# Retention in a two-layer hybrid trunk: outputs parked in their queries' place, normalised two tiles at a time, transposed five steps on, and the PSUM bank `o` used in halves

## The chip, the cores and the metric

The kernel runs on one core of a Trainium2 chip. The metric is device time in microseconds (us) for one execution; a kernel's time is the median of its runs. One more execution was taken with the hardware profiler, and every row shown here comes from it.

## The reference, cut to what matters

The program is one inference step of a trunk of two layers over 1280 tokens: 1024 latent tokens and 256 context tokens, 1024 channels, float32. Every layer normalises and modulates its input, multiplies it by one wide input matrix, runs three token mixers side by side (a retention of 4 heads in both directions, grouped-query attention, latent attention), multiplies their outputs by a gate, and projects back. The change lies in the retention, and in a PSUM bank that retention and both attentions share. What the retention must give, for each chunk of 128 tokens:

```python
def step(s, inp):
    qi, ki, vi = inp
    a = jnp.einsum('bihd,bjhd->bhij', qi, ki) * intra
    o = (jnp.einsum('bhij,bjhe->bihe', a, vi)
         + jnp.einsum('bihd,bhde->bihe', qi, s) * q_dec[None, :, :, None])
    s = s * c_dec[None, :, None, None] + jnp.einsum('bjhd,bjhe->bhde', ki * k_dec[None, :, :, None], vi)
    return s, o
...
o = rms_norm(o_f + jnp.flip(o_b, 1))      # over the 64 columns of each head
```

## The kernel before

The tokens are 10 tiles of 128 rows (`NT` = 10; tiles 0 to 7 latent, 8 and 9 context). One SBUF tensor `yxs` holds all of them; `yx[t]` is tile t, 1024 columns wide, and its first 256 columns hold the retention's queries until the retention's output takes their place.

A layer's second half of the input projection is the gate: `z_blk` runs four times, each with two column blocks by three token blocks (512, 512 and 256 tokens), and each such block is 24 matmuls (lines 685 to 687) into a bank `acc`. Scalar engine then takes a tanh (line 690) and vector engine a product (line 692) out of that bank, in two halves. These matmuls need nothing from the mixers, so other work is woven between them: `aside()` is a generator, and `z_blk` draws one step from it after, and in wide blocks also in the middle of, each block, 40 draws in all. What it yields in order: the rest of the key transposes, the latent keys and values (`latents`), the retention (10 steps that gather the states `S`, then the steps t = 0, 1, 2, ... of the main loop), and the attention's preparation (loads and splits of its first keys and values, then the first three score jobs, lines 1249 and 1250), three of its steps at a draw. A scheduler orders the instructions of each engine by priority and by its own estimate of when their inputs are there; each engine then runs its list strictly in that order, and waits on semaphores.

One step t of the retention's main loop works on three tiles:

- `stage_c(t-2)`: eight pairs of small matmuls (lines 905, 906) put the outputs of tile t-2 into the left half of PSUM bank `o`; scalar engine squares them into the right half (line 907); vector engine sums the squares per head (909), computes the reciprocal root by Newton steps on 128x4 elements (`newton`, lines 152 to 162: 13 small instructions), and multiplies the outputs by it into an SBUF tile `oret` (912). The next tile's outputs go into the same bank.
- `stage_b(t-1)`: two matmuls (895) give the scores of tile t-1; vector engine multiplies them by the decay mask into `At` (897).
- `stage_a(t)`: gpsimd has doubled the queries into `qq` (401); PE transposes them (870) and the keys (873), vector engine makes the decayed queries `qdT` (877), scalar engine copies queries and keys into `BD` and `kT` (879, 880, 882). In the free half of the keys' bank PE transposes `oret` of tile t-3 (`stage_d`, 918), and scalar engine copies it to `yx` (919).

The banks `pt`, `pk` and that of line 895 come from one ring `tp` of two banks, so the key transposes of step t (873) take the bank out of which line 897 reads the scores of tile t-1. `qq` and `At` share a ring `kd` of three buffers.

In the attention, `pv_job` accumulates the outputs of one head over two token tiles in the left half of bank `o` (lines 1313, 1314); scalar engine copies 64 of its rows (1325) and vector engine adds the other 64 (1326). Then the next pair of tiles may start in that bank.

Of the kernel before, what the change touches and what calls it, by code (L numbers as in the profile page):

```python
# [10 lines left out]
F32 = mybir.dt.float32  # L11
# [7 lines left out]
P = 128  # L19
# [63 lines left out]
def hybrid_trunk(tc, I, O):  # L83
# [51 lines left out]

    def bank(tag):
        if tag == "o":
            return pp.tile([P, 512], F32, name=tag, tag=tag, bufs=1)
        if tag == "m":
            tag = "tp"  # L140
        bufs = {"acc": NACC, "tp": 7 - NACC}[tag]
        return pp.tile([P, 512], F32, name=tag, tag=tag, bufs=bufs)
# [647 lines left out]
    def retention(l, rt, load, kv):  # L790
# [76 lines left out]
        def stage_a(t, kv, qq):  # L867
# [6 lines left out]
            if t >= 3:  # L874
                stage_d(t - 3, outs.pop(t - 3), pk[:, 256:512])
# [24 lines left out]
        def stage_c(t, kv, qdT, At):  # L900
            bo = bank("o")
            po, sq = bo[:, 0:256], bo[:, 256:512]
            for h in range(4):
                hs = slice(h * 64, (h + 1) * 64)
                T.matmul(po[:, hs], At[:, h, :], kv[:, 256 + h * 64:256 + (h + 1) * 64], start=True, stop=False)  # L905
                T.matmul(po[:, hs], qdT[:, h, :], S[:, t, hs], start=False, stop=True)  # L906
            A.activation(sq, po, AF.Square)
            ss = sm.tile([P, 4], F32, name="ss4", tag="ss4")
            V.tensor_reduce(ss, h4(sq), axis=AX.X, op=ALU.add)
            rstd = newton(ss, 4, 1.0 / 64)  # L910
            o = rt.tile([P, 256], F32, name="oret", tag="cur", bufs=2)
            V.tensor_tensor(h4(o), h4(po), bc(rstd), op=ALU.mult)
            return o

        def stage_d(t, o, pt):

            for i in range(2):
                T.transpose(pt[:, i * 128:(i + 1) * 128], o[:, i * 128:(i + 1) * 128], ident)
            A.copy(yx[t][:, 0:256], pt)

        st, At, outs = {}, {}, {}
        for t in range(NT + 3):
            yield
            if 2 <= t < NT + 2:
                outs[t - 2] = stage_c(t - 2, st[t - 2][0], st[t - 2][1], At.pop(t - 2))
# [8 lines left out]
            elif t >= 3:  # L934
                stage_d(t - 3, outs.pop(t - 3), bank("tp")[:, :256])
# [126 lines left out]
    def attention(l, att):  # L1062
# [207 lines left out]
        def exp_job(p, i, b, ps):  # L1270
# [3 lines left out]
            if b == p.nb - 1 and i == 1:  # L1274
                if p.i not in ris:
                    ris[p.i] = sm.tile([P, 5, 2, 2], F32, name="ri", tag="ri", bufs=3)
# [27 lines left out]
        def pv_job(p, b, c0, c1):  # L1304
            if b == 0 and c0 == 0:
                p.po = bank("o")[:, :256]
# [415 lines left out]
```

## Time and profile before

| | us |
|---|---|
| median of 3 runs | 2138.68 |
| lowest and highest run | 2135.28 and 2139.26 |
| the profiled execution | 2134.77 |
| its span, first to last instruction | 2133.0 |

The profiled execution is 3.9 us below the median, about as far as the lowest run. Of its time 1.8 us lie outside the span.

| engine | busy us | share of the span |
|---|---|---|
| PE (TensorE matmul) | 2064.7 | 97% |
| DVE (vector) | 1489.9 | 70% |
| ACT (scalar) | 1177.9 | 55% |
| POOL (gpsimd) | 992.8 | 47% |

The granted TensorE clock was 0.994 of full speed as a mean, and 1.00 in the stretches spoken of here. Each engine's idle time is put down to what ended it, so that a row of the waits says who waited, on which line, for whom, how long in total, how many times, and the longest. The retention's main part lies at 405 to 487 us of the span in the first layer and at 1430 to 1515 us in the second.

### The profile page before, as it was taken

The numbers are of one execution on the slowest core, as the hardware profiler recorded it, in microseconds if no ns is written. First come the engines' busy times: TensorE is split into PE (matmuls) and PEld (weight loads), VectorE is DVE, ScalarE is ACT, GpSimd is POOL, SyncE is SP. The second block draws the span as 40 slices with busy tenths as digits, with TensorE's granted clock in tenths as the row PEclk, the third lists the DMA queues.
The fourth block names the chain that finished last, engine by engine and source line by source line (L and its number), as shares of the span: only waits on it lengthen the run. The fifth ranks groups of instructions, "written<-read, shape, count | busy, mean of one in ns | idle before, by whom it ended". The sixth has DMA issues, their size and how long they took to land. (4 is left out here: it accounts for less than half of the span.)

```text
span 2133.0 us, 42211 instructions
## 1 busy us (share of the span) xinstructions
PE 2064.7 (97%) x14798; PEld 1854.8 (87%) x14798; DVE 1489.9 (70%) x3780; ACT 1177.9 (55%) x3190; POOL 992.8 (47%) x1444
## 2 busy tenths in 40 slices
PE   6999999999999999999999999998999999999998
PEld 3899987778888888888999999887788888888898
DVE  4625584566999999997174358546699999999824
ACT  3503333225888888885253233322388888888623
POOL 2342242325676565544543224223275766564474
PEclk9999999999999999999999999999999999999999
DMA  9442436414111110014143212452321111010322
GB/s 323 138 150 60 132 105 197 137 49 121 34 52 34 31 48 27 24 35 149 41 157 106 62 55 57 135 148 74 98 61 30 40 48 41 12 40 24 108 94 100
DMA packets 203814, 179.94 MB, mean 84 GB/s; under 512 B 37532, under 2 KB 186324, under 8 KB 203604
## 3 DMA queue, kind: packets, MB, share of 16 engines
q1 hardware_dynamic: 202164, 172.01, 26.9%
q10 hardware_dynamic: 1440, 5.24, 0.6%
q8 instruction: 118, 1.93, 0.4%
q14 instruction: 92, 0.75, 0.1%
HBM read 131.32 MB, written 45.86 MB: 83 GB/s over the span
## 5 line engine op out<-in xcount | busy, mean ns | idle before, releaser
L258 PE MATMUL acc<-wh,ah 128*128 128x256 f32 (+1 forms) x1760 | 504.0, 286 | 1.8 <-ACT ah L406 1.8
L260 PE MATMUL acc<-wh,al 128*128 128x256 f32 (+1 forms) x1760 | 500.5, 284 | 2.6 <-DVE al L407 2.4
L259 PE MATMUL acc<-wl,ah 128*128 128x256 f32 (+1 forms) x1760 | 501.7, 285 | 0.0
L1258 DVE TENSOR_REDUCE nm<-acc 128x1 f32<-128x512 f32 (+1 forms) x624 | 413.7, 666 | 47.1 <-PE acc L1252 34.0
L1297 PE MATMUL tp<-ident,pn 128*128 128x128 f32 x2400 | 433.6, 274 | 3.9 <-DVE pT L1302 2.3
L1302 DVE TENSOR_TENSOR pT<-tp,pT 128x512 fp32r<-128x512 f32 (+1 forms) x624 | 412.7, 663 | 27.8 <-ACT pT L1301 19.4
L1272 ACT ACTIVATE pn<-acc,nm 128x512 f32<-128x512 f32 (+1 forms) x624 | 421.2, 682 | 10.2 <-DVE nm L1263 9.3
L1301 ACT CAST pT<-tp 128x512 fp32r<-128x512 f32 (+1 forms) x624 | 356.4, 573 | 122.9 <-PE tp L1297 117.5
L258 PEld LDWEIGHTS acc<-wh,ah 128*128 128x128 f32 x1760 | 335.1, 190 | 13.1 <-issue 7.8
L260 PEld LDWEIGHTS acc<-wh,al 128*128 128x128 f32 x1760 | 333.5, 190 | 4.9 <-DVE al L407 4.3
L259 PEld LDWEIGHTS acc<-wl,ah 128*128 128x128 f32 x1760 | 334.3, 190 | 0.8 <-issue 0.8
L1313 PE MATMUL o<-pT,V 128*128 128x256 f32 x1200 | 326.2, 293 | 1.5 <-DVE yx L1326 1.5
L1297 PEld LDWEIGHTS tp<-ident,pn 128*128 128x128 f32 x2400 | 287.5, 140 | 35.9 <-PE acc L1250 7.4
L1314 PE MATMUL o<-pT,V 128*128 128x256 f32 x1200 | 312.1, 282 | 0.0
L1313 PEld LDWEIGHTS o<-pT,V 128*128 128x128 f32 x1200 | 226.6, 189 | 19.9 <-DVE yx L1326 6.0
L1314 PEld LDWEIGHTS o<-pT,V 128*128 128x128 f32 x1200 | 226.4, 189 | 17.8
L194 POOL TENSOR_SCALAR wh<-raw 128x512 fp32r<-128x512 f32 (+2 forms) x144 | 81.8, 578 | 323.4 <-PE acc L260 144.3
L195 POOL TENSOR_TENSOR wl<-raw,wh 128x512 fp32r<-128x512 f32 (+2 forms) x144 | 164.0, 1151 | 5.2
L1249 PE MATMUL acc<-K,Qm 128*128 128x512 f32 (+1 forms) x312 | 143.3, 459 | 0.0
L685 PE MATMUL acc<-ah,wh 128*128 128x512 f32 (+1 forms) x384 | 140.5, 366 | 0.0
L686 PE MATMUL acc<-ah,wl 128*128 128x512 f32 (+1 forms) x384 | 139.2, 362 | 0.0
L1250 PE MATMUL acc<-K,Qm 128*128 128x512 f32 (+1 forms) x312 | 138.7, 444 | 0.0
(283 smaller groups left out, 3869.6 us busy)
## 6 DMA issues: line engine op xcount, KB each, us to landing
raw<-in_w_ada_dram SPq DMA_DIRECT2D x96, 256.0 KB, 3.2
raw<-in_w_in_dram SPq DMA_DIRECT2D x56, 256.0 KB, 2.9
kv<-s_rkv SPq DMA_DIRECT2D x40, 256.0 KB, 3.0
s_gT<-eo SPq DMA_DIRECT2D x80, 128.0 KB, 2.1
yx<-in_x_sample_dram SPq DMA_DIRECT2D x16, 512.0 KB, 6.6
gt<-s_gT SPq DMA_DIRECT2D x60, 128.0 KB, 2.6
raw<-in_w_in_dram SPq DMA_DIRECT2D x56, 128.0 KB, 2.3
rb<-s_sum SPq DMA_DIRECT2D x100, 64.0 KB, 2.7
```

The lines of the kernel that those rows point to most:

```text
L195: G.tensor_tensor(wl, raw, wh.bitcast(F32), op=ALU.subtract)
L258: T.matmul(ps, ah[:, k, :], wh, start=(k == 0), stop=False)
L259: T.matmul(ps, ah[:, k, :], wl, start=False, stop=False)
L260: T.matmul(ps, al[:, k, :], wh, start=False, stop=(k == KC - 1))
L1249: T.matmul(ps, p.Q[:, 0, qs], K, start=True, stop=False)
L1258: V.tensor_reduce(nm[:, b:b + 1], ps, axis=AX.X, op=ALU.max, negate=True)
L1272: A.activation(pn, ps, AF.Exp, bias=p.ng[i], accum_out=p.su[:, i, b:b + 1])
L1297: T.transpose(pt[:, c * 128:(c + 1) * 128], pn[:, c * 128:(c + 1) * 128], ident)
L1301: A.copy(ph, p3)
L1302: V.tensor_tensor(pl, p3, ph.bitcast(F32), op=ALU.subtract)
L1313: T.matmul(p.po, vc, p.gran[b][:, 0, c, :], start=(ch == 0), stop=False)
L1314: T.matmul(p.po, vc, p.gran[b][:, 1, c, :], start=False, stop=(ch == last))
```

## The change

- Bank `o` becomes one tile that is held for the whole program; each call of `bank("o")` hands out the other half of it, 256 columns.
- `stage_c` squares the outputs into an SBUF tile `sq` (ring `cur`, where `oret` was) and copies them as they are to `yx[t][:, 0:256]`, the place of their queries: one more scalar instruction a tile, 20 in all.
- The sums of squares of two tiles go side by side into a 128x8 tile; `newton` runs once for both, after the odd tile (10 runs in place of 20, so 130 small vector instructions fewer), and two vector multiplications normalise both tiles in place in `yx`.
- `stage_d` transposes tile t-5 in step t, out of `yx` and no longer out of `oret`; the main loop has 15 steps in place of 13.
- The ring `ri` of the attention's row sums has 2 buffers in place of 3.

```diff
@@ -133,9 +133,13 @@
     for j in (32, 96):
         V.memset(lo_rows[j:j + 32, :], -1.0)
 
+    o_bank = pp.tile([P, 512], F32, name="o")
+    o_turn = [0]
+
     def bank(tag):
         if tag == "o":
-            return pp.tile([P, 512], F32, name=tag, tag=tag, bufs=1)
+            o_turn[0] ^= 1
+            return o_bank[:, 256 * o_turn[0]:256 * o_turn[0] + 256]
         if tag == "m":
             tag = "tp"
         bufs = {"acc": NACC, "tp": 7 - NACC}[tag]
@@ -871,8 +875,8 @@
             pk = bank("tp")
             for j in range(2):
                 T.transpose(pk[:, j * 128:(j + 1) * 128], kv[:, j * 128:(j + 1) * 128], ident)
-            if t >= 3:
-                stage_d(t - 3, outs.pop(t - 3), pk[:, 256:512])
+            if t >= 5:
+                stage_d(t - 5, pk[:, 256:512])
             qdT = rt.tile([P, 4, 128], F32, name="qdT", tag="qdT", bufs=2)
             V.tensor_tensor(qdT.rearrange("p h c -> p (h c)"), pt, decT.rearrange("p h c -> p (h c)"), op=ALU.mult)
             pq = pt.rearrange("p (j x c) -> p x j c", j=2, x=2)
@@ -898,31 +902,36 @@
             return At
 
         def stage_c(t, kv, qdT, At):
-            bo = bank("o")
-            po, sq = bo[:, 0:256], bo[:, 256:512]
+            po = bank("o")
             for h in range(4):
                 hs = slice(h * 64, (h + 1) * 64)
                 T.matmul(po[:, hs], At[:, h, :], kv[:, 256 + h * 64:256 + (h + 1) * 64], start=True, stop=False)
                 T.matmul(po[:, hs], qdT[:, h, :], S[:, t, hs], start=False, stop=True)
+            sq = rt.tile([P, 256], F32, name="sq", tag="cur", bufs=2)
             A.activation(sq, po, AF.Square)
-            ss = sm.tile([P, 4], F32, name="ss4", tag="ss4")
-            V.tensor_reduce(ss, h4(sq), axis=AX.X, op=ALU.add)
-            rstd = newton(ss, 4, 1.0 / 64)
-            o = rt.tile([P, 256], F32, name="oret", tag="cur", bufs=2)
-            V.tensor_tensor(h4(o), h4(po), bc(rstd), op=ALU.mult)
-            return o
-
-        def stage_d(t, o, pt):
+            A.copy(yx[t][:, 0:256], po)
+            if t % 2 == 0:
+                sums.append(sm.tile([P, 8], F32, name="ss8", tag="ss8", bufs=2))
+            V.tensor_reduce(sums[0][:, t % 2 * 4:t % 2 * 4 + 4], h4(sq), axis=AX.X, op=ALU.add)
+            if t % 2:
+                rstd = newton(sums.pop(), 8, 1.0 / 64)
+                for u in range(2):
+                    o = h4(yx[t - 1 + u][:, 0:256])
+                    V.tensor_tensor(o, o, bc(rstd[:, 4 * u:4 * u + 4]), op=ALU.mult)
+
+        sums = []
+
+        def stage_d(t, pt):
 
             for i in range(2):
-                T.transpose(pt[:, i * 128:(i + 1) * 128], o[:, i * 128:(i + 1) * 128], ident)
+                T.transpose(pt[:, i * 128:(i + 1) * 128], yx[t][:, i * 128:(i + 1) * 128], ident)
             A.copy(yx[t][:, 0:256], pt)
 
-        st, At, outs = {}, {}, {}
-        for t in range(NT + 3):
+        st, At = {}, {}
+        for t in range(NT + 5):
             yield
             if 2 <= t < NT + 2:
-                outs[t - 2] = stage_c(t - 2, st[t - 2][0], st[t - 2][1], At.pop(t - 2))
+                stage_c(t - 2, st[t - 2][0], st[t - 2][1], At.pop(t - 2))
             if 1 <= t <= NT:
                 At[t - 1] = stage_b(st[t - 1][2])
             if t < NT:
@@ -931,8 +940,8 @@
                     doubled(t + 1)
                 st[t] = stage_a(t, kv, qqs.pop(t))
                 kv = nx_kv
-            elif t >= 3:
-                stage_d(t - 3, outs.pop(t - 3), bank("tp")[:, :256])
+            elif t >= 5:
+                stage_d(t - 5, bank("tp")[:, :256])
 
     def cache_keys(l, pool, bufs):
 
@@ -1273,7 +1282,7 @@
             p.pn[i, b] = pn
             if b == p.nb - 1 and i == 1:
                 if p.i not in ris:
-                    ris[p.i] = sm.tile([P, 5, 2, 2], F32, name="ri", tag="ri", bufs=3)
+                    ris[p.i] = sm.tile([P, 5, 2, 2], F32, name="ri", tag="ri", bufs=2)
                 ri = ris[p.i][:, p.pr, :, p.mla]
                 if p.nb > 1:
                     V.tensor_reduce(ri, p.su[:, :, 0:p.nb], axis=AX.X, op=ALU.add)
@@ -1303,7 +1312,7 @@
 
         def pv_job(p, b, c0, c1):
             if b == 0 and c0 == 0:
-                p.po = bank("o")[:, :256]
+                p.po = bank("o")
             last = p.nb * p.nch - 1
             while (p.i not in MV) if p.mla else p.i // 3 not in GV:
                 step(True)
```

Line numbers move on: 895 becomes 899, 897 becomes 901, 905 and 906 become 908 and 909, 907 is 911, 909 is 915, 912 is 920, 918 is 927, 685 to 687 are 689 to 691, 1249 and 1250 are 1258 and 1259. PE, POOL and the DMA queue have as many instructions as before, POOL in the same order; outside of the gate's stretch no engine's order changes.

**PE, second output group of the retention's main loop (step t = 3, layer 0).** `o` is the bank of outputs, `tp` the ring of two banks, `acc` a gate bank; in brackets stands whose semaphore an instruction waits for. Before:

```order
L895 MATMUL tp<-BD,kT 128x256 [waits PE_49,Activation_49]
L895 MATMUL tp<-BD,kT 128x256
L870 MATMUL tp<-ident,qq 128x128 [waits DVE_49,Pool_49]
L870 MATMUL tp<-ident,qq 128x128 x2
L905 MATMUL o<-kv,At 128x64 [waits DVE_49]
L906 MATMUL o<-S,qdT 128x64
```

Now:

```order
L877 MATMUL tp<-ident,kv 128x128
L690 MATMUL acc<-ah_130,wl 128x512
L691 MATMUL acc<-al_131,wh 128x512
L908 MATMUL o<-kv,At 128x64 [waits Activation_49]
L909 MATMUL o<-S,qdT 128x64
```

The outputs of tile 1 stand ahead of the scores and the query transposes of their step, and they wait for the scalar engine, where they waited for the vector engine. The group of tile 0, which uses the other half and is the first user, has no such wait in either kernel.

**PE, what follows an output group (end of the group of tile 1, layer 0), now:**

```order
L909 MATMUL o<-S,qdT 128x64
L899 MATMUL tp<-BD,kT 128x256 [waits PE_49,Activation_49]
L899 MATMUL tp<-BD,kT 128x256
L874 MATMUL tp<-ident,qq 128x128 [waits DVE_49,Pool_49]
L874 MATMUL tp<-ident,qq 128x128 x3
L689 MATMUL acc<-ah_130,wh 128x512
L690 MATMUL acc<-ah_130,wl 128x512
L877 MATMUL tp<-ident,kv 128x128 [waits DMAHW1_49,DVE_49]
```

The scores of the next tile follow at once, and the key transposes, which wait for the vector engine, stand two gate matmuls behind the query transposes.

**DVE, the same step.** Before, from the normalisation of tile 0 on:

```order
L912 TENSOR_TENSOR oret<-o,nwy 128x256 [waits DVE_49,Pool_49]
L897 TENSOR_TENSOR At<-tp,MT 128x512 [waits PE_49,Pool_49]
L877 TENSOR_TENSOR qdT<-tp,decT 128x512 [waits PE_49]
L909 TENSOR_REDUCE ss_5666<-o 128x4 [waits Activation_49]
L152 TENSOR_SCALAR nwx<-ss_5666 128x4 [waits DVE_49]
```

Now, from the sum of squares of tile 1 on:

```order
L915 TENSOR_REDUCE ss_5595<-sq 128x4 [waits Activation_49]
L156 TENSOR_SCALAR nwx<-ss_5595 128x8 [waits DVE_49]
L901 TENSOR_TENSOR At<-tp,MT 128x512 [waits PE_49,Pool_49]
L157 TENSOR_SCALAR nwu<-nwx 128x8 [waits DVE_49]
L881 TENSOR_TENSOR qdT<-tp,decT 128x512 [waits PE_49]
```

The masked scores `At`, which stood behind the normalisation, now stand behind the sum of squares of the tile before, and in this step behind the first Newton instruction too. In tiles 3 and 5 the three stand in the same order; in tile 7 `At` stands ahead of the Newton instruction, and in the even tiles there is none.

**PE, end of the gate's stretch (layer 0).** `Q` and `K` are the attention's first queries and keys. Before:

```order
L687 MATMUL acc<-al_130,wh 128x512
L1249 MATMUL acc<-K,Q_6396 128x512 [waits DVE_49,Pool_49]
L1249 MATMUL acc<-K,Q_6396 128x512 [waits DVE_49,PE_49] x2
L685 MATMUL acc<-ah_131,wh 128x512 [waits DVE_49]
L686 MATMUL acc<-ah_131,wl 128x512
```

Now:

```order
L691 MATMUL acc<-al_133,wh 128x512
L1258 MATMUL acc<-K,Q_6345 128x512 [waits DVE_49,PE_49,Pool_49]
L1258 MATMUL acc<-K,Q_6345 128x512 [waits DVE_49,PE_49]
L1258 MATMUL acc<-K,Q_6345 128x512 [waits DVE_49]
L689 MATMUL acc<-ah_134,wh 128x256 [waits DVE_49,PE_49]
```

The first three score jobs stood ahead of the last 512-wide gate block, and stand one block later, ahead of the last, 256-wide one.

## Rows read from the trace of the kernel before

**Rows 1.** The page's first part: busy us (share of span), instructions.

```profile
PE 2064.7 (97%) x14798; PEld 1854.8 (87%) x14798; DVE 1489.9 (70%) x3780; ACT 1177.9 (55%) x3190; POOL 992.8 (47%) x1444
```

**Rows 2.** PE's waits, whole span: line, releaser: us in total, times, longest.

```profile
PE o L905 <- DVE oret L912: 10.2, 12, 1.2
...
PE tp L870 <- POOL qq L401: 2.6, 2, 1.3
...
PE tp L873 <- DVE At L897: 1.8, 2, 0.9
...
PE o L1313 <- DVE yx L1326: 1.5, 3, 0.7
...
PE tp L918 <- DVE oret L912: 0.5, 2, 0.3
```

**Rows 3.** Windows, both retention stretches: us, busy by engine, clock, DMA share, GB/s.

```profile
405.00:487.00 82.00, 74.00 (x475) 63.25 (x474) 52.15 (x184) 22.21 (x64) 28.03 (x46) 1.00 0.20 61
...
1430.00:1515.00 85.00, 76.87 (x487) 65.58 (x486) 52.68 (x185) 22.15 (x65) 27.99 (x46) 1.00 0.21 62
```

**Rows 4.** PE's timeline, layer 0: start us, us, instruction [idle before, releaser].

```profile
425.84 0.28 PE L870 MATMUL tp<-ident,qq 128*128 128x128 f32 x1
...
428.26 0.40 PE L687 MATMUL acc<-al,wh 128*128 128x512 f32 x1
428.49 1.02 PE L895 MATMUL tp<-BD,kT 128*128 128x256 f32 x4
...
429.71 0.48 PE L685 MATMUL acc<-ah,wh 128*128 128x512 f32 x1
430.03 0.40 PE L686 MATMUL acc<-ah,wl 128*128 128x512 f32 x1
431.33 0.44 PE L873 MATMUL tp<-ident,kv 128*128 128x128 f32 x2 [0.90 <-DVE At L897]
...
458.08 1.02 PE L895 MATMUL tp<-BD,kT 128*128 128x256 f32 x4
```

**Rows 5.** DVE's timeline, the same stretch.

```profile
426.76 0.41 DVE L909 TENSOR_REDUCE ss<-o 128x4 f32<-128x256 f32 x1
427.21 0.17 DVE L152 TENSOR_SCALAR nwx<-ss 128x4 f32<-128x4 f32 x1
427.41 0.73 DVE L153 TENSOR_SCALAR nwu<-nwx 128x4 int32<-128x4 int32 x1
...
430.60 0.68 DVE L897 TENSOR_TENSOR At<-tp,MT 128x512 f32<-128x512 f32 x1
431.20 0.41 DVE L912 TENSOR_TENSOR oret<-o,nwy 128x256 f32<-128x256 f32 x1
...
454.56 0.42 DVE L909 TENSOR_REDUCE ss<-o 128x4 f32<-128x256 f32 x1 [2.21 <-ACT o L907]
454.91 0.68 DVE L897 TENSOR_TENSOR At<-tp,MT 128x512 f32<-128x512 f32 x1
...
459.14 0.69 DVE L897 TENSOR_TENSOR At<-tp,MT 128x512 f32<-128x512 f32 x1 [0.31 <-PE tp L895]
```

**Rows 6.** ACT's timeline: squares of two tiles.

```profile
426.09 0.37 ACT L907 ACTIVATE o<-o 128x256 f32<-128x256 f32 x1 [4.33 <-PE o L906]
...
454.16 0.37 ACT L907 ACTIVATE o<-o 128x256 f32<-128x256 f32 x1 [2.70 <-PE o L906]
```

**Rows 7.** POOL's timeline behind the same output group.

```profile
426.69 0.61 POOL L827 TENSOR_TENSOR cur<-S,cdec 64x256 f32<-64x256 f32 x1 [0.21 <-POOL qq L401]
...
427.38 0.74 POOL L828 TENSOR_TENSOR S<-S,cur 64x256 f32<-64x256 f32 x1
```

**Rows 8.** ACT's timeline, end of the gate's stretch: last key copy, first exponential.

```profile
511.34 0.40 ACT L1149 CAST kpr<-st 128x256 fp32r<-128x256 f32 x1
...
514.18 0.68 ACT L1272 ACTIVATE pn<-acc,nm 128x512 f32<-128x512 f32 x1
```

**Rows 9.** PE's timeline there: the first score job behind the gate's last matmul.

```profile
514.46 0.47 PE L1249 MATMUL acc<-K,Q 128*128 128x512 f32 x1 [0.66 <-DVE eo L692]
```

**Rows 10.** DVE's timeline there: three row maxima of score jobs.

```profile
515.20 1.89 DVE L1258 TENSOR_REDUCE nm<-acc 128x1 f32<-128x512 f32 x3 [0.47 <-PE acc L1250]
```

## The prediction, made before the changed kernel was timed

> **What bounds the kernel now.** I read the busy shares first: PE is busy for 2064.7 us of a span of 2133.0 us, 97%, and no other engine is over 70% [rows 1]. So PE sets the time, the change removes no PE instruction, and all it can give is part of PE's 68.3 idle us. The table of PE's waits says where those are: the largest single row is the outputs of the retention (line 905) waiting for the normalisation (line 912), 10.2 us in 12 waits; the transposes of the outputs wait 0.5 us for the same line, and the key transposes (873) 1.8 us for the masked scores [rows 2]. The windows confirm the place: PE is idle for 82.00 - 74.00 = 8.0 us in the first layer's stretch and 85.00 - 76.87 = 8.1 us in the second's, while DVE is busy for 52 of some 83 us [rows 3]. DVE is not short of time there; it is late because its work for one tile is a chain. The timeline shows it: an output group is followed by PE's next instruction at 425.84 [rows 4], the square starts at 426.09 [rows 6], the sum of squares at 426.76, then come the Newton steps, and only at 431.20 the multiplication that reads the bank for the last time [rows 5]. A step lasts about 6.95 us (the sums of squares at 426.76 and 454.56 are four tiles apart), and the next group, due earlier in it, waits for this.
>
> I call T0 the time at which PE issues its first instruction behind an output group.
>
> **The change part by part.**
>
> *The bank's release.* A tile's outputs now leave the bank by two scalar instructions, square and copy, of about 0.37 us each: the square starts at T0 + 0.25 (425.84 to 426.09) and takes 0.37 [rows 4, 6], and a copy of 128x256 out of PSUM is a row of the same shape, so the bank is read out at about T0 + 1.0. The next group comes over 4 us after T0. This wait goes wholly: 10.2 + 0.5 us [rows 2]. Cover is ample: were the copy late by 3 us, nobody would notice.
>
> *The halves.* They bring nothing by themselves, I think. In the new order the second output group, which writes the half that nobody has used, still waits for the scalar engine, whose only work on the bank by then is to read the other half: the program guards the bank as one. So in the attention too a pair still waits for the last reader of the pair before, and the 1.5 us there [rows 2] stay. No row shows two engines in two halves at once. The Trainium skill, page "PSUM — Partial Sum Buffer", section "PSUM bank collisions raise a hardware error", says that two engines in the same bank and the same 32 partitions collide even at different columns, and that one has to guard by bank, not by address. By that rule the halves cannot be used at once and the sum below stands; were it otherwise, the sum would be 1.5 us better, which is the third rival.
>
> *The extra copies, the saved Newton runs, the two more steps.* 20 scalar copies lie on an engine busy for 22 of 82 us in the stretch [rows 3]; the 130 vector instructions saved were on the chain that goes anyway; the transposes move, two a tile as before, and read `yx`, ready two steps earlier. No PE time in any of it. Nor in `ri`: a head's sums are read out two pairs before the third head begins.
>
> *What is late next: the masked scores.* The key transposes take their bank out of the ring of two, so they wait until the masked scores are read. Before, this wait was hidden behind the one on the outputs but for 0.9 us a layer, where the masked scores started at 430.60 behind the Newton steps [rows 5, 4]. That row goes too: 1.8 us. In its place stands a new chain: behind an output group PE does the score matmuls, the query transposes and two gate matmuls, then the key transposes. The rows of that same sequence: scores at 428.49, two gate matmuls at 429.71 and 430.03, key transposes due at 431.33 - 0.90 = 430.43, which is T0 + 1.94 [rows 4]. The masked scores start 0.04 us behind the end of the score matmuls (458.08 + 1.02 = 459.10, and 459.14 on DVE) and take 0.69, and PE starts 0.05 after their end (430.60 + 0.68 = 431.28, and 431.33) [rows 4, 5]: with DVE free, T0 + 1.02 + 0.04 + 0.69 + 0.05 = T0 + 1.80, in time.
> But DVE is not free: the sum of squares stands ahead. It starts 0.40 us behind the square (454.16, 454.56) and lets the next instruction start 0.35 us later (454.91) [rows 6, 5]: T0 + 0.25 + 0.40 + 0.35 = T0 + 1.00, just ahead of T0 + 1.06. Even tiles therefore wait between 0 and 0.2 us; I take 0.06 for each of the 5 steps a layer without a Newton instruction in the way, 0.6 us in all.
> In tiles 1, 3 and 5 the first Newton instruction stands in the way too. It starts 0.45 us behind the sum of squares (426.76, 427.21), T0 + 1.10, and holds DVE for 0.20 us (427.21 to 427.41) or, where it meets a gpsimd instruction, as its neighbour did at 427.41, for 0.73 [rows 5, 7]. The masked scores then start at T0 + 1.30 to 1.83 and the key transposes at T0 + 2.04 to 2.57: a wait of 0.10 to 0.63. I take 0.35, since gpsimd's instruction at 426.69 to 427.30 [rows 7] lies over T0 + 1.10 (426.94) and ends 0.36 us later. Three tiles in two layers: 2.1 us (0.6 to 3.8).
>
> *The end of the gate's stretch.* The retention ends two draws later, so the attention's preparation does, and the first three score jobs stand a block later. Before, the last key copy starts at 511.34 and the first exponential at 514.18 [rows 8], and the next score job waited 0.66 us for a bank [rows 9]. Now three row maxima, 1.89 us [rows 10], fall into the last block with the key copies and the gate's products. A 512-wide matmul keeps PE for 0.23 us (428.26 to 428.49 [rows 4]); the last block's 24 are half as wide, so about 0.12 us each, and with six score matmuls PE has some 4.3 us there (an estimate); DVE has the 1.89 and about 2 us of products and copies to do in it. I charge 0.5 us a layer, 1.0 us in all; the bounds are a gain of 0.66 us a layer, if that wait goes, and a loss of 1.89, if the maxima come wholly behind the gate.
>
> *Left as they are:* the query transposes' wait for gpsimd, 2.6 us [rows 2], because POOL's order is the same.
>
> *Sum.* 10.2 + 0.5 + 1.8 = 12.5 us go; 2.1 + 0.6 + 1.0 = 3.7 us come. Net 8.8 us: 2134.77 - 8.8 = 2126.0 us for the profiled execution. It was 3.9 us under the median of 2138.68; from the median the forecast is **2129.9 us**, 0.4% faster.
>
> **The rivals.**
>
> *The wait moves to the vector engine.* For it: DVE and ACT run in order, and a tanh that waits for a gate product behind 13 Newton instructions holds up the next square, and with it the sum of squares and the masked scores. Against it: from T0 + 2.2, the end of the masked scores, the decayed queries (0.7), eleven instructions at 0.2 and two multiplications at 0.4 end at about T0 + 6.0, before the next group does. If every step pays the 0.63 us bound, 8 steps in two layers cost 10.1 us; with 1.0 us at the end, 12.5 - 11.1 = 1.4 us are left: 2137.3 us, no change.
>
> *The preparation comes too late, and the kernel is slower.* Place: the border of gate and attention. Two draws are one wide block, 24 matmuls at 0.23 us [rows 4] = 5.5 us. If the chain of loads, splits, three score jobs and maxima is bound by the landing of its loads, it slides by all of that: the last key copy at 511.34 + 5.5, 3 us past the gate's end, then the maxima, 1.89 us, before the first exponential. Two layers: 2 x (5.5 + 1.9) = 14.8 us, with the masked scores 2.7 us, against 12.5: 2138.68 + 5.0 = 2143.7 us. It decides from about 5 us a layer. Against it: POOL's and DVE's work in the stretch also comes earlier, since the retention ends some 5 us sooner.
>
> *The halves do serve.* If pairs really overlap, the 1.5 us of the attention [rows 2] go as well, and the end costs nothing: 12.5 + 1.5 - 2.7 = 11.3 us, 2127.4 us.
>
> **How the numbers follow.** The forecast has 0.68, the wait that moves 0.18, the late preparation 0.08, the serving halves 0.06. The measurement can tell about 0.2%, 4.3 us, from no change. Forecast and halves lie beyond it on the fast side: faster 0.74, same 0.18, slower 0.08. The range: at best 12.5 + 1.5 - 0.6 + 1.3 = 14.7 us less, 2124.0 us; upwards it takes in most of the rival at 2137.3 and leaves out the slow one: 2124 to 2137 us.
>
> **What would show it.** In the profile after, right: no row in which the outputs (908) wait for a normalisation; key transposes (877) waiting for line 901 for 1 to 5 us in all; the two retention stretches with 3 to 4 us of PE idle time each in place of 8; the attention's line 1322 waiting as before. Wrong: key transposes that wait over 8 us, as in the first rival; over 3 us more PE idle time a layer between the last gate block and the first transposes of the attention, as in the second; no wait at 1322, as in the third; or idle time in a stretch that the change doesn't touch.

## The result and the profile after

The changed kernel takes 2115.07 us (median of 4 runs, 2114.37 to 2116.68); the kernel before, run beside it, takes 2137.69 us (4 runs, 2135.28 to 2139.26). The ratio is 0.9898, with a 95% interval of 0.9886 to 0.9909: 1.0% faster, 22.6 us, where 8.8 us were forecast, and below the low end of the range, 2124. In the later sets of runs the kernel before has a median of 2135.9 to 2136.3 us over 7 to 15 runs, so the gain is rather 21 us: the median of three runs on which the forecast was set, 2138.68, was some 2.6 us high.

The page's first part, after (busy us, share of the span of 2112.9 us, instructions), answers [rows 1]:

```profile
PE 2057.3 (97%) x14798; PEld 1852.3 (88%) x14798; DVE 1459.5 (69%) x3650; ACT 1184.1 (56%) x3210; POOL 993.1 (47%) x1444
```

PE's busy time fell by 7.4 us, although it issues the same 14,798 matmuls. That is the first thing that the prediction has no term for: it counted only PE's idle time. PE's waits after (as in [rows 2]), with that of the score jobs behind the gate (line 1249, now 1258):

```profile
PE tp L874 <- POOL qq L405: 2.6, 2, 1.3
...
PE o L1322 <- DVE yx L1335: 1.3, 2, 0.7
...
PE acc L1258 <- DVE eo L696: 1.0, 2, 0.5
```

No row is left in which the outputs (908), their transposes (927) or the key transposes (877) wait for DVE: of 10.2 + 0.5 + 1.8 us nothing stays. Where the time went is seen in windows that hold the same work: in each layer the same 600 matmuls, in a partly different order, from one in the gate's first block (line 685, now 689; in the second layer its neighbour on line 687, now 691) to a matmul of the attention behind the gate (a score job, line 1249, now 1258; in the second layer a transpose on line 1297, now 1306). The kernel before (columns as in [rows 3]):

```profile
411.42:521.81 110.39, 100.98 (x603) 84.85 (x601) 71.93 (x224) 38.39 (x103) 40.08 (x64) 1.00 0.30 87
1439.27:1549.70 110.43, 100.95 (x602) 84.95 (x601) 72.53 (x223) 38.50 (x102) 39.95 (x64) 1.00 0.31 89
sum 220.82, PE 201.93 PEld 169.79 DVE 144.46 ACT 76.89 POOL 80.03; mean PE 100.97 PEld 84.90 DVE 72.23 ACT 38.44 POOL 40.01
```

and the changed kernel:

```profile
412.08:514.61 102.53, 99.47 (x602) 84.77 (x600) 57.29 (x159) 41.38 (x113) 39.61 (x65) 1.00 0.32 94
1427.86:1530.31 102.45, 99.41 (x603) 84.81 (x601) 57.47 (x158) 41.37 (x112) 39.55 (x65) 1.00 0.33 95
sum 204.98, PE 198.88 PEld 169.59 DVE 114.76 ACT 82.74 POOL 79.16; mean PE 99.44 PEld 84.79 DVE 57.38 ACT 41.37 POOL 39.58
```

The two stretches lost 220.82 - 204.98 = 15.8 us: 12.8 us of PE's idle time (18.9 to 6.1) and 3.05 us of what is counted as busy. The clock is 1.00 in all four windows. I read most of the 3.05 us as the hidden part of the waits. One wait of the kernel before on PE's timeline:

```profile
437.11 0.48 PE L685 MATMUL acc<-ah,wh 128*128 128x512 f32 x1
438.65 0.43 PE L905 MATMUL o<-kv,At 128*128 128x64 f32 x2 [1.07 <-DVE oret L912]
```

The gate matmul starts at 437.11, and its record lasts to 437.59; from there the idle time of 1.07 us is counted. But where nothing is waited for, the matmul behind such a 512-wide one with a record of 0.48 us starts after 0.32 us (429.71 and 430.03 in [rows 4]; after 0.23 us where the record is 0.40, as at 428.26 and 428.49), here at 437.43. So this wait cost 438.65 - 437.43 = 1.22 us, 0.15 more than listed. The three rows of [rows 2] that went have 16 waits, all in the stretches. Read in this way from PE's timelines, each against the pace of the kind of matmul ahead of it, they cost 15.1 us where 12.5 are listed: 2.6 us more, 0.16 for each. The other 0.4 of the 3.05 us I don't place. The Trainium skill, page "Perfetto Trace Analysis", section "Tensor Engine Instruction (MATMUL, LD_WEIGHTS)", says that the profile's end of a matmul is an estimate from its size, "a model, not a measurement"; the rows agree, since work that waits for nothing starts 0.23 us after a start whose record lasts 0.40, and 0.32 us after one whose record lasts 0.48.

I call an interval from start to start less such a pace **by starts**. The output groups alone cost 6.0 us a layer by starts; the 6.9 us in the expectation of no_newton are too high.

The new wait that the prediction charged at the key transposes, after an output group. PE of the changed kernel (layer 0):

```profile
435.73 1.08 PE L899 MATMUL tp<-BD,kT 128*128 128x256 f32 x4
...
437.31 0.40 PE L690 MATMUL acc<-ah,wl 128*128 128x512 f32 x1
437.69 0.33 PE L877 MATMUL tp<-ident,kv 128*128 128x128 f32 x1
```

and DVE:

```profile
436.40 0.42 DVE L915 TENSOR_REDUCE ss<-sq 128x4 f32<-128x256 f32 x1 [4.31 <-ACT sq L911]
436.86 0.17 DVE L156 TENSOR_SCALAR nwx<-ss 128x8 f32<-128x8 f32 x1
436.94 0.69 DVE L901 TENSOR_TENSOR At<-tp,MT 128x512 f32<-128x512 f32 x1
437.55 0.24 DVE L157 TENSOR_SCALAR nwu<-nwx 128x8 int32<-128x8 int32 x1
```

T0 is 435.73 here. The first Newton instruction does stand ahead of the masked scores, but they start 0.08 us behind it (436.86 to 436.94), not 0.20 to 0.73. The 0.20 us of [rows 5] are the distance to an instruction that needs its result, and the masked scores don't. The 0.73 us are those of an instruction that meets a gpsimd instruction, and here gpsimd's is all but over (436.34 to 436.95). It is the same in all six places, three tiles in two layers: gpsimd stands still or ends within 0.1 us, the Newton instruction's record lasts 0.17 us, and the masked scores start 0.08 us behind it. A slow one would hold them up: in one_by_one, below, a Newton instruction that meets gpsimd takes 0.64 us, and the masked scores behind it start after 0.56 us, although they don't need its result.

```profile
417.59 0.64 DVE L157 TENSOR_SCALAR nwu<-nwx 128x4 int32<-128x4 int32 x1
418.15 0.68 DVE L901 TENSOR_TENSOR At<-tp,MT 128x512 f32<-128x512 f32 x1
```

The key transposes start at T0 + 1.96, 0.38 us behind the gate matmul, so 0.15 us by starts; it lies under that matmul's record, and the profile lists nothing. They are late by 0.12 to 0.15 us at four places in each layer, 1.1 us in all.

### The profile page after: what moved, and what is told of

Same layout as the page of the kernel before. It is cut to its first block, busy times and chain, and to the rows that moved or that the text cites. A ratio compares the mean times of both kernels' runs of the same rounds, so it can differ in the third digit from the quotient of the medians.

```text
span 2112.9 us, 42103 instructions
## 1 busy us (share of the span) xinstructions
PE 2057.3 (97%) x14798; PEld 1852.3 (88%) x14798; DVE 1459.5 (69%) x3650; ACT 1184.1 (56%) x3210; POOL 993.1 (47%) x1444
## 3 DMA queue, kind: packets, MB, share of 16 engines
q8 instruction: 118, 1.93, 0.4%
## 4 chain that ended last, share of the span: by engine, by line
PE 76%; DVE 3%; ACT 1%; issue 1%; POOL 1%; DMA 1%; SPq 0%; DVEq 0%; POOLq 0%; ACTq 0%
PE tp L1306 13%; PE o L1322 7%; PE acc L1258 7%; PE o L1323 7%; PE acc L1259 6%; PE acc L264 6%; PE acc L263 6%; PE acc L262 6%; PE acc L1261 3%; PE acc L691 3%; PE acc L689 3%; PE acc L690 3%; PE o L909 1%; PE tp L840 1%; PE o L908 1%
## 5 line engine op out<-in xcount | busy, mean ns | idle before, releaser
L691 PE MATMUL acc<-al,wh 128*128 128x512 f32 (+1 forms) x384 | 138.6, 361 | 0.0
```

## The experiments

The stretches are those of the windows above, between the same matmuls. "Before" is the kernel before, run on the same chip in the same set.

| kernel | median us | before us | ratio, 95% interval | stretches us |
|---|---|---|---|---|
| changed | 2115.07 | 2137.69 | 0.9898 (0.9886 to 0.9909) | 102.53, 102.45 |
| no_newton | 2117.77 | 2136.30 | 0.9911 (0.9896 to 0.9925) | 102.53, 102.47 |
| copy_alone | 2122.42 | 2136.03 | 0.9932 (0.9919 to 0.9945) | 105.45, 105.11 |
| one_by_one | 2119.27 | 2136.03 | 0.9917 (0.9905 to 0.9930) | 103.75, 103.66 |
| three_steps | 2117.65 | 2135.87 | 0.9911 (0.9897 to 0.9924) | 104.29, 104.30 |
| four_steps | 2117.80 | 2136.30 | 0.9911 (0.9895 to 0.9928) | 103.77, 103.72 |
| one_half | 2115.55 | 2136.03 | 0.9903 (0.9886 to 0.9919) | 102.56, 102.50 |
| halves_alone | 2136.58 | 2136.03 | 0.9998 (0.9989 to 1.0007) | 111.52, 110.17 |
| two_sums | 2135.95 | 2135.87 | 0.9997 (0.9988 to 1.0006) | 110.56, 110.41 |
| queries_on_act | 2115.76 | 2135.87 | 0.9901 (0.9887 to 0.9915) | 102.69, 102.52 |
| scores_first | 2116.24 | 2135.87 | 0.9904 (0.9889 to 0.9919) | 102.92, 102.83 |

### The wait alone: no_newton

```diff
-            rstd = newton(ss, 4, 1.0 / 64)
+            rstd = sm.tile([P, 8], F32, name="nwy", tag="nwy")[:, :4]
+            V.tensor_scalar(rstd, ss, 0.0, 0.125, op0=ALU.mult, op1=ALU.add)
```

> The kernel before with the Newton steps of the retention's normalisation left out: one vector instruction gives a constant in place of 13, so the outputs are scaled wrongly; bank, copies, pairs and steps are those of before. This takes away the wait alone: the bank is read out some 1.5 us behind the output group. Theory (by starts, the ten output groups of a layer cost PE 6.9 us in the kernel before, the listed idle time of 10.2 us in both layers leaving out what lies under the record of the matmul ahead): the stretches get 7.5 to 8.5 us shorter in each layer, as in the changed kernel, 2115 to 2120 us. Rival (the listed idle time is the price: 10.2 + 1.8 + 0.5 = 12.5 us at most, the rest of the changed kernel's gain comes from its other parts): 2123.5 us or above, stretches 6.2 us shorter at most.

The sum of the stretches' windows:

```profile
sum 205.00, PE 199.40 PEld 170.28 DVE 96.75 ACT 77.21 POOL 79.63; mean PE 99.70 PEld 85.14 DVE 48.37 ACT 38.61 POOL 39.81
```

205.00 us against 204.98 in the changed kernel. With bank, copies and steps of before, and nothing but a short chain on DVE, both stretches are as short as in the changed kernel: 15.8 us is what DVE's chain cost PE there, where the three listed rows add up to 12.5. PE's busy time falls by 2.5 us with it, from 201.93. The rival, which takes the listed idle time for the price, is out. One thing is not held fixed: the scheduler builds another order around the shorter chain, and most output groups now stand behind a gate matmul, as in the changed kernel, so the 15.8 us are those of the chain together with the order that goes with it.

### The copy alone, and tiles one by one: copy_alone, one_by_one

copy_alone, from the kernel before (the square goes to SBUF too, and the multiplication works in place):

```diff
+            sq = rt.tile([P, 256], F32, name="sq", tag="cur", bufs=2)
             A.activation(sq, po, AF.Square)
+            A.copy(yx[t][:, 0:256], po)
...
-            o = rt.tile([P, 256], F32, name="oret", tag="cur", bufs=2)
-            V.tensor_tensor(h4(o), h4(po), bc(rstd), op=ALU.mult)
+            o = yx[t][:, 0:256]
+            V.tensor_tensor(h4(o), h4(o), bc(rstd), op=ALU.mult)
```

> The kernel before with one part of the change: the scalar engine copies a tile's outputs out of the bank to their queries' place and the square goes to SBUF; every tile is still normalised by itself, and transposed three steps on. Theory (PE loses, at each output group, the time from one start to the next, which is more than the idle time that the profile lists, since a matmul's record ends later than the next one could start: by starts the ten groups of each layer cost 6.6 to 6.8 us more in the kernel before than in the changed one, 13.4 us in both layers, and the profile lists 10.2): most of the whole gain is here, 15 to 20 us, 2118 to 2123 us. Rival (the copy gives what the profile lists, 10 to 12 us, less the masked scores' new wait behind Newton's first instruction in every tile, and normalising in pairs gives the rest): 2127 to 2131 us.

one_by_one, from the changed kernel:

```diff
...
-            if t % 2:
-                rstd = newton(sums.pop(), 8, 1.0 / 64)
...
+            rstd = newton(ss, 4, 1.0 / 64)
...
```

> The changed kernel with every tile normalised by itself (13 vector instructions for each tile again), five steps kept. Theory (an independent instruction starts 0.08 us behind Newton's first one, so that hardly holds up the masked scores): 2115 to 2117 us, key transposes late by about 0.15 us in eight tiles of a layer by their starts, and no idle row for it. Rival (normalising in pairs carries part of the gain; by the price in the prediction 0.35 us for each of the five or so tiles more in each layer, or by its bound 0.63): 2119 to 2122 us.

copy_alone gains 13.6 us, 10.3 of them in the stretches: two thirds of the changed kernel's gain. Its time lies at the slow end of what the theory said, its gain just under the 15 to 20 us. The outputs wait no more; the two other rows, 1.8 and 0.5 us in [rows 2], have grown, each with one wait in a layer as before (waits of PE, whole span):

```profile
PE tp L873 <- DVE At L897: 2.4, 2, 1.4
...
PE tp L919 <- DVE yx L913: 2.1, 2, 1.0
```

one_by_one has five steps, loses the second of them, and keeps the first:

```profile
PE tp L877 <- DVE At L901: 2.2, 2, 1.1
```

Here my theory was wrong by 2 us or more: I had the price of normalising every tile small everywhere, and it is, but for one place in each layer. The rival's time came true, but not its reason, a price on every further tile. At that place PE has (one_by_one, first layer):

```profile
422.22 1.08 PE L899 MATMUL tp<-BD,kT 128*128 128x256 f32 x4
...
425.54 0.44 PE L877 MATMUL tp<-ident,kv 128*128 128x128 f32 x2 [1.11 <-DVE At L901]
```

and DVE:

```profile
420.83 0.56 DVE L166 SCALAR_TENSOR_TENSOR nwy<-nwu,nwy 128x4 f32<-128x4 f32 x1
421.42 0.16 DVE L164 TENSOR_TENSOR nwu<-nwy 128x4 f32<-128x4 f32 x1
421.62 0.58 DVE L165 TENSOR_TENSOR nwu<-nwu,nwx 128x4 f32<-128x4 f32 x1
...
423.77 0.78 DVE L917 TENSOR_TENSOR yx<-yx,nwy 128x256 f32<-128x256 f32 x1
...
424.81 0.67 DVE L901 TENSOR_TENSOR At<-tp,MT 128x512 f32<-128x512 f32 x1
```

and gpsimd:

```profile
420.76 0.60 POOL L831 TENSOR_TENSOR cur<-S,cdec 64x256 f32<-64x256 f32 x1
421.44 0.73 POOL L832 TENSOR_TENSOR S<-S,cur 64x256 f32<-64x256 f32 x1
```

The next scores are there at 423.30, but the Newton run of the first output group and its multiplication hold DVE until 424.5, since many of the small instructions take 0.46 to 0.65 us here, where gpsimd works almost without a gap, and 0.16 elsewhere. Each of these slow ones ends 0.01 to 0.03 us behind the end of a gpsimd instruction (420.83 + 0.56 = 421.39 on DVE, 420.76 + 0.60 = 421.36 on gpsimd). The masked scores start at T0 + 2.6 (422.22 to 424.81) in place of T0 + 1.2. The Trainium skill, page "GPSIMD Engine Reference", section "1. Specifications", says that GpSimd's SBUF interfaces are shared with VectorE, with contention for DVE instructions in a 2-port perf mode or with two SBUF inputs; the slow rows shown here read two tiles each and agree with it. Two with a single input, on lines 157 and 158, took as long (0.64 and 0.65 us); whether they ran in such a mode no row shows. In the changed kernel the first tile has no Newton steps of its own, and this wait is not there. So a wait can move to DVE, as the prediction's first rival has it, though by a shorter way than its tanh and at one place only: it costs 1.2 us a layer in the stretches (103.7 against 102.5), and the pairing takes it away.

### The steps: three_steps, four_steps

three_steps, from the changed kernel; the main loop has 13 steps again, and four_steps has 4 for 3 and 14 steps:

```diff
-            if t >= 5:
-                stage_d(t - 5, pk[:, 256:512])
+            if t >= 3:
+                stage_d(t - 3, pk[:, 256:512])
...
-        for t in range(NT + 5):
+        for t in range(NT + 3):
...
```

> The changed kernel with the transposes three steps on, as before, instead of five; tiles still normalised in pairs. Theory (an even tile is normalised in the same step in which it is transposed: DVE ends that pair 5.4 us behind the output group, and the transposes stand some 2 us behind it): a wait of about 3 us in four or five tiles of each layer, less what the order lets slide, 10 to 30 us slower than the changed kernel, 2125 to 2145 us. Rival (the steps are free, DVE is in time): 2115 to 2118 us.

> The changed kernel with the transposes four steps on instead of five: an even tile is then transposed in the step behind the one that normalises it, and the retention ends one draw earlier. Theory (the wait of the last transposes for the normalisation, 1.3 us a layer with three steps, goes with one step more; one draw at the end is worth nothing): 2114 to 2117 us, stretches at 102.5 us each as in the changed kernel. Rival (the fifth step is needed, the transposes still wait): stretches of 103.5 us or more, 2117 us or above.

three_steps missed its 10 to 30 us by far: it is 2.6 us slower than the changed kernel, within the rival's range, and its two stretches are 3.6 us longer. Its built order does not leave the transposes of an even tile where they would wait 3 us; it puts them into the next output group, where they go through without a listed wait. In both kernels one group of transposes near the end of each layer's retention waits for DVE, 2.0 us listed in three_steps and 2.2 in four_steps (`PE tp L927 <- DVE yx L920: 2.2, 2, 1.1`). PE in four_steps:

```profile
475.50 0.40 PE L691 MATMUL acc<-al,wh 128*128 128x512 f32 x1
477.01 0.44 PE L927 MATMUL tp<-ident,yx 128*128 128x128 f32 x2 [1.11 <-DVE yx L920]
```

By starts that is 477.01 - 475.50 - 0.23 = 1.28 us, again 0.17 more than listed, and 2 x 1.28 = 2.6 us is just what four_steps is longer than the changed kernel in the two stretches (207.49 - 204.98 = 2.5). The theory of four_steps (one more step suffices) falls; the fifth step is what that group needs.

### The halves: halves_alone, one_half

halves_alone, from the kernel before:

```diff
+    o_bank = pp.tile([P, 512], F32, name="o")
...
-                p.po = bank("o")[:, :256]
+                o_turn[0] ^= 1
+                p.po = o_bank[:, 256 * o_turn[0]:256 * o_turn[0] + 256]
```

> The kernel before, with the bank of outputs given out in halves in the attention alone; the retention still takes the whole bank, and every engine's order is that of before. Theory (the gain lies in the two retention stretches, where the outputs no longer wait): no change, 2137.7 us within 2 us, and the attention's output matmuls wait for the last reader of the pair before, 1.5 us in all, as before. Rival (the halves give part of it): the changed kernel's attention took about 1 us less in each layer than that of before between the same matmuls; if that comes from the halves, this kernel is about 2 us faster, 2135.5 us, and that row of waits shrinks.

one_half, from the changed kernel:

```diff
-            o_turn[0] ^= 1
-            return o_bank[:, 256 * o_turn[0]:256 * o_turn[0] + 256]
+            return o_bank[:, 0:256]
```

> The changed kernel, with one and the same half of the bank given out every time; the order of every engine is that of the changed kernel. Theory (halves bring nothing): 2115.1 us within 2 us, no row in which the outputs wait for the copy of the tile before, attention as in the changed kernel. Rival (the halves give part of the gain): outputs and pairs wait for the reader of the bank, 2 us or more are lost, 2117 us or above.

Both went as the theory had it: halves alone change nothing, and without them nothing is lost. The attention's wait stays in halves_alone,

```profile
PE o L1317 <- DVE yx L1330: 1.5, 3, 0.7
```

as in [rows 2]. (Its first stretch is 1.1 us longer than that of before, at a granted clock of 0.98: from 480.9 to 484.3 us PE was granted 0.50, the lower of its two levels, shortly behind an output group's wait of 1.18 us; the kernel before has the same wait and keeps 1.00.)

### The buffer of row sums: two_sums

```diff
-                    ris[p.i] = sm.tile([P, 5, 2, 2], F32, name="ri", tag="ri", bufs=3)
+                    ris[p.i] = sm.tile([P, 5, 2, 2], F32, name="ri", tag="ri", bufs=2)
```

> The kernel before, with two buffers instead of three for the sums of the attention's heads; every engine's order is that of before. It is about 2 us that the changed kernel gains in the attention, over the same matmuls in the same order (886.5 us in both layers, 888.7 before; 886.5 with one half, 887.3 with tiles normalised one by one, 888.8 with the copy alone, which keeps three buffers). Theory (these 2 us have nothing to do with that buffer): attention at 888.7 us, time within 2 us of before. Rival (they come from the buffer, the only edit in the attention that those kernels share): attention at 886.5 to 887.5 us, time 1 to 2 us under before.

The same attention matmuls of both layers, as sums of windows of the kernel before, of two_sums, and of the changed kernel:

```profile
sum 888.69, PE 887.05 PEld 786.75 DVE 810.76 ACT 753.39 POOL 533.97; mean PE 443.52 PEld 393.37 DVE 405.38 ACT 376.70 POOL 266.99
```

```profile
sum 887.58, PE 885.86 PEld 786.96 DVE 810.64 ACT 754.12 POOL 534.51; mean PE 442.93 PEld 393.48 DVE 405.32 ACT 377.06 POOL 267.25
```

```profile
sum 886.53, PE 884.89 PEld 786.08 DVE 810.70 ACT 753.33 POOL 532.92; mean PE 442.44 PEld 393.04 DVE 405.35 ACT 376.67 POOL 266.46
```

Half of the 2.2 us comes with the buffer alone in this execution, but two_sums' whole time can't be told from that of before. The other traces say more: over the same matmuls the four kernels with three buffers take 888.7 to 889.1 us (before, halves_alone, copy_alone, no_newton), the eight with two take 886.5 to 887.6. So the microseconds go with the buffer, whatever the retention does. They are spread thinly over thousands of matmuls, most over the attention's output matmuls (lines 1313 and 1314: 1.4 of the 1.9 us between the means of the two groups), and no wait that shrinks stands behind them. By what way a smaller ring does this stays open; the changed kernel with three buffers was not run.

### What is late next: queries_on_act, scores_first

queries_on_act, from the changed kernel:

```diff
-                pin(pool_copy(qqs[t], h4(yx[t][:, 0:256]).unsqueeze(2).to_broadcast([P, 4, 2, 64])))
+                copy = A.copy if t == 2 else pool_copy
+                pin(copy(qqs[t], h4(yx[t][:, 0:256]).unsqueeze(2).to_broadcast([P, 4, 2, 64])))
```

> The changed kernel with the doubled queries of the third tile copied by ACT instead of POOL. The query transposes wait there for POOL, 1.3 us in each layer, since POOL splits weights first; ACT is idle. Theory (PE loses from start to start 1.68 us there where 0.22 is the pace, 1.46 us a layer): the wait goes, 2.9 us less than the changed kernel, 2112.2 us. Rival (by the listed idle time, or with something else late next, such as the key transposes or the key copy behind it on ACT): 0 to 2.6 us less, 2112.5 to 2115 us.

The query transposes' 2.6 us went, and nothing was gained: the next key transposes wait as long.

```profile
423.80 0.41 PE L878 MATMUL tp<-ident,kv 128*128 128x128 f32 x2 [1.43 <-DVE nwy L166]
```

The profile names a Newton instruction, but no key transpose needs one; the masked scores had been done since 422.3 (421.60, 0.68 us long). What they also need is the load of the tile, issued only at 420.45 behind weight loads on SP's queue (below). The trace has its landing: the last of its 16 parts at 423.66, and the first key transpose starts at 423.80. In the changed kernel the same load lands at 423.80, too, but the key transposes start only at 425.29.

```profile
419.80 0.60 SPq L229 DMA_DIRECT2D raw<-in_w_out_dram  x1
420.45 1.06 SPq L790 DMA_DIRECT2D kv<-s_rkv  x2
```

scores_first, from the changed kernel: the sum of squares and what follows is issued behind `stage_b`, and pinned there:

```diff
+        def stage_c2(t, sq):
...
-            V.tensor_reduce(sums[0][:, t % 2 * 4:t % 2 * 4 + 4], h4(sq), axis=AX.X, op=ALU.add)
+            pin(V.tensor_reduce(sums[0][:, t % 2 * 4:t % 2 * 4 + 4], h4(sq), axis=AX.X, op=ALU.add))
...
+            if 2 <= t < NT + 2:
+                stage_c2(t - 2, sq)
```

> The changed kernel with the sum of squares put behind the masked scores on DVE. Theory (the masked scores come 0.15 us later than PE could use them in four tiles of a layer, seen from start to start as 0.36 us ahead of the key transposes where 0.23 is the pace, and listed as no idle time): these intervals fall to 0.23 to 0.25, about 1.1 us less in both layers, 2114 us, at the edge of what the timing can tell. Rival (the masked scores aren't what these intervals wait for, or the later sum holds up the normalisation and the last transposes): intervals stay at 0.36, 2115 to 2117 us.

The rival is right: the interval ahead of the key transposes stays at 0.35 us (436.46 to 436.81 on its PE timeline), although DVE now has nothing ahead of the masked scores and waits for the scores' matmuls:

```profile
436.07 0.69 DVE L901 TENSOR_TENSOR At<-tp,MT 128x512 f32<-128x512 f32 x1 [4.32 <-PE tp L899]
436.67 0.41 DVE L918 TENSOR_REDUCE ss<-sq 128x4 f32<-128x256 f32 x1
```

T0 is 434.88: start at T0 + 1.19, where the changed kernel has 1.21 with the sum and a Newton instruction ahead. Those two cost 0.02 us. None of the kernels is measurably faster than the changed one.

## Why the prediction was wrong, point by point

**What bounds the kernel, and where the change acts**: right. PE's idle time in the two retention stretches is what went, and DVE's chain behind one output group was its cause (no_newton).

**The price of the removed waits, 12.5 us: too low by 2.6.** This is the first step that failed. All three rows went, as forecast, but a wait costs PE its listed idle time and the time that lies under the record of the matmul ahead, 0.16 us for each of the 16 waits: 15.1 us. no_newton and the changed kernel agree on 15.8 us for both stretches as a whole.

**What comes in its place, 3.7 us: 1.1 us, and not for the reasons given.** The second step that failed. Listed idle time fell by 12.8 us in the stretches, the whole 12.5, so none of the charges shows up there. The 2.1 us for Newton's first instruction took 0.20 us, the distance of two dependent instructions, or 0.73 beside gpsimd, for what it would hold up the masked scores; it was 0.08, since they don't need its result and gpsimd was out of the way in time. The 0.6 us for the sum of squares: with sum and Newton instruction ahead the masked scores start 0.02 us later than with nothing ahead, by scores_first. What is left is that the key transposes are late by some 0.15 us by starts at four places a layer, with a free DVE too. A chain of T0 + 1.80 was worked out, and T0 + 1.93 to 1.96 is measured: behind an output group the score matmuls take 1.08 us and not 1.02, and the masked scores start 0.11 us behind their end in scores_first, not 0.04. And T0 + 1.94, when the key transposes were said to be due, was counted from a matmul's modelled end, as the waits were; by starts PE could have begun them at 430.03 + 0.23 = 430.26, T0 + 1.77. The 1.0 us at the end of the gate's stretch: the score jobs' wait for the gate's product fell from 1.3 to 1.0 us, so no loss came (before, the same view has `PE acc L1249 <- DVE eo L692: 1.3, 2, 0.7`).

So the stretches give 12.5 - 3.7 = 8.8 in the forecast. Measured are 15.8: 15.1 for the waits, less 1.1 for the late key transposes, and 1.8 us more, 0.3 of them idle time of the score jobs. The rest I take to lie in the other order of the matmuls; I have not traced it further.

**Outside the stretches, 0: 2.2 us in the attention**, which go with the buffer `ri` in all twelve traces. The prediction costed it at nothing, by an argument on when a buffer comes free; how the time is saved is not explained. Of the 20.1 us between the two profiled spans (2133.0 and 2112.9) 15.8 + 2.2 = 18.0 are then placed. The last 2.1 us lie in work that both kernels issue in the same order: 2133.0 - 220.8 - 888.7 = 1023.5 us before and 2112.9 - 205.0 - 886.5 = 1021.4 after. In two_sums, where that work is the same, it takes 2135.2 - 221.0 - 887.6 = 1026.6. Two executions differ by more than is left over, so I don't put it down to the change.

**The halves bring nothing**: right, by both kernels, and the attention's wait is there as before (1.3 and 1.5 us). The third rival is out.

**The extra copies and the two more steps cost no PE time**: right. What the prediction didn't see is that they are not free to leave out: four steps cost 2.5 us and single tiles 2.4 us in the stretches. It had the saved Newton runs "on the chain that goes anyway"; in one place a layer they aren't.

**The rivals.** The wait that moves to DVE didn't come in the changed kernel, but a shorter form of it does in one_by_one and copy_alone, at one place in a layer rather than at every step. The late preparation didn't come: the score jobs' wait behind the gate got shorter.

**The range** failed with the terms: its best case, 14.7 us, took the listed rows as the most that could be won.

**What would show it**: no row of 908, and 1322 waiting as before, both as written; the 1 to 5 us of key transposes waiting for 901 didn't appear. For the retention stretches 3 to 4 us of PE idle time each were written, in place of 8. Over as many matmuls as in the windows of [rows 3], counted from the same first one, it is 1.9 us each (74.73 - 72.86 and 77.49 - 75.63): less than written, since the charged waits show no idle time.

```profile
405.87:480.60 74.73, 72.86 (x475) 63.59 (x473) 39.12 (x122) 26.61 (x76) 27.69 (x46) 1.00 0.25 72
1418.75:1496.24 77.49, 75.63 (x487) 65.83 (x486) 39.21 (x122) 26.43 (x76) 27.69 (x46) 1.00 0.25 72
```

The 3.1 and 3.0 us of the longer windows above stand against 9.4 and 9.5 before.

## What to carry to other kernels

Price a wait of PE from start to start, against the pace of the same matmul where nothing is waited for: the listed idle time begins at a modelled end, and was a sixth short here, 12.5 us of 15.1. Take the pace from the same record length, since 0.23 and 0.32 us both occur behind matmuls of one shape. Before you charge an instruction that is queued ahead of another, look whether the interval that you take for it lies between dependent instructions, and whether gpsimd is busy beside it. And when a wait goes, see which load or copy ends just behind it: here 2.6 us on the next row were worth nothing.

## What the runs showed of the hardware that I had not expected

A vector instruction that doesn't need the result of the one ahead starts some 0.08 us before that one's record ends: 0.08 us behind a 128x8 instruction of 0.17 us, 0.56 us behind a 128x4 one of 0.64 us. And in one_by_one each small vector instruction that took 0.46 to 0.65 us beside gpsimd ended 0.01 to 0.03 us behind a gpsimd instruction, so that its length says when gpsimd ended, and little of its own work. Two halves of one bank gave nothing in either kernel: the attention's wait for the other half's reader stayed at 1.5 us in halves_alone, since the program guards the bank as a whole; whether engines could work in both at once was not tried.
